# Context heads of three attention groups: transposed by VectorE in 32x32 blocks, their values summed on eight 32x64 tiles

## The chip, the cores and the metric

The kernel runs on one core of one Trainium2 chip. The metric is the device time of one execution in microseconds. The engines are named as the profile names them: PE is the matrix engine (PEld its weight loads), DVE the vector engine, ACT the scalar engine, POOL the GpSimd engine, and SP the engine that issues most DMAs.

## The reference

One layer of a diffusion transformer for 128 context tokens and 512 latent tokens, all float32, width 1024. Each of the two kinds of token is normalised and modulated, multiplied with one wide matrix `w_in`, and goes through grouped attention and a short gated convolution; then comes a gated feed-forward part. There are 16 query heads in 4 groups; the 4 heads of a group share one key and one value head of 64 columns. What matters here is the attention, and in it the context tokens, which read context tokens only:

```python
def block_attention(q, k, v):
    ...
    def one_block(qblk):
        s = jnp.einsum('bqkgd,btkd->bkgqt', qblk, k).astype(jnp.float32) * scale
        p = jax.nn.softmax(s, axis=-1).astype(v.dtype)
        return jnp.einsum('bkgqt,btkd->bqkgd', p, v)
    ...
# in the layer
h_p, k_ctx, v_ctx = trunk_layer(h_p, ada_ctx, p, None, None, None)
h_s, _, _ = trunk_layer(h_s, ada_lat, p, rope_tabs, cache_k[:, i], cache_v[:, i])
```

For a group the context part is thus four 128x128 score matrices (128 queries, 128 keys), a softmax over the keys, and four products with the same 128x64 matrix V. Latent queries read 640 keys: 128 cached ones and the 512 latent ones. The context's keys and values are outputs too (`new_k`, `new_v`).

## The kernel before

All 640 tokens (128 context, then 512 latent) are held on the chip with features on the partitions. Weights arrive in tiles of 128x1024 float32 (`raw`, three buffers) and are split into a rounded high part (ACT, `whi`) and the remainder (DVE, `wlo`), so that a product is three passes of the reduced-precision matmul (`mm3`, lines 157 to 159). Softmax weights and V are multiplied as plain float32, which the trace shows as two records for each matmul.

The attention stage goes over the groups `g` = 0 to 3, and in each over nine steps `i`. Step 0 makes the scores of the context heads (`Step(g)`, 4 heads, 128x128 each); steps 1 to 8 make those of two latent heads for 128 queries (`Step(g, place)`, two heads, 128x640 each, line 589). A step's scores are reduced to a maximum on DVE (`most`, lines 722, 727 and 729) and turned into exponentials with their sum on ACT (`exps`, lines 736 and 742); `shares` divides by the sum (reciprocal on DVE, lines 747 and 751; product on POOL, lines 748 and 752). One step later `turned` transposes the result on PE so that the keys lie on the partitions (context: line 760, latent: line 765), and a copy brings it from PSUM to the tile `PT` (line 762 on ACT, line 770 on ACT or DVE). `values` multiplies it with V (context: line 780, in step 2 of the group; latent: line 789, in steps 4, 6, 8 and step 1 of the next group), and its result is split into `AH` (ACT, line 794) and `AL` (DVE, line 795), the operands of the output projection.

The order of instructions on PE, ACT and DVE is the order in which the program writes them; the scheduler orders only SP and POOL and sets the waits and the buffers. In each step other PE work is written between the parts: half of a query projection for the next group (`q_part`), the other half, transposes of turned queries (`q_turn`, line 560), and modulation matmuls (`ada_mm`, line 209). Weight loads go through a ring (`ring_load`, lines 139 and 203) on SP. Remainders of the weights of the next projections are made in between on DVE (`cut_hi`, lines 690 and 693).

PSUM in this stage has two pools: `ps2()` gives tiles of two banks, of which there are three, and `ps1()` gives tiles of one bank, of which there are two:

```python
def ps2():
    return ps.tile([128, 1024], F32, tag="s2", name=nm("s2"), bufs=3)
def ps1():
    return psa.tile([128, 512], F32, tag="s1", name=nm("s1"), bufs=2)
```

The scores of a latent step take two tiles of `ps2`, those of the context step one; each transposed result takes one tile of `ps2`; `values` takes one of `ps1`. A tile is given again when the instructions that read it are done. `VV[:, 5]` holds V of the context tokens, with the 128 keys on the partitions and 4x64 columns for the four groups. `k_double(0)` also issues the DMAs that write `new_v` and `new_k` (lines 660 and 661).

Of the kernel before, what the change touches and what calls it, by code (L numbers as in the profile page):

```python
# [11 lines left out]
F32 = mybir.dt.float32  # L12
F32R = mybir.dt.float32r
AF = mybir.ActivationFunctionType
ALU = mybir.AluOpType
# [46 lines left out]
def trunk_layer(ctx, tc, x_prompt, x_sample, cache_k, cache_v, c, c_ctx, w_ada, b_ada, g_pre1, g_post1, g_pre2,  # L62
                g_post2, w_in, q_norm, k_norm, w_att_out, conv_w, w_conv_out, w_o, w_up, conv_ffn, w_down, rope,
                y_prompt, y_sample, new_k, new_v):
    nc = tc.nc
    V, S, G, PE = nc.vector, nc.scalar, nc.gpsimd, nc.tensor
# [17 lines left out]
    dp = ctx.enter_context(tc.tile_pool(name="dp", bufs=1, space=bass.MemoryType.DRAM))  # L84
# [7 lines left out]
    def nm(s):  # L92
        cnt[0] += 1
        return f"{s}_{cnt[0]}"

    def region(pool, tag, shape, dtype, name):
        return pool.tile([128] + shape, dtype, tag=tag, name=name)
# [6 lines that stand above are left out]
# [82 lines left out]
    scsh = const.tile([128, KT, 4], F32, name="scsh")  # L186
    mod = const.tile([128, 4, 2, KT], F32, name="mod")
    bct = dp.tile([64, 128], F32, name="bct")
    hd = dp.tile([NT, 128, D], F32, name="hd")
    actd = dp.tile([NJ, 128, NACT], F32, name="actd")  # L190

# [73 lines left out]
    with tc.tile_pool(name="pro", bufs=2) as pro, tc.manual_schedule(engines={mybir.EngineType.SP}):  # L265
# [122 lines left out]
        VV = kvp_.tile([128, 6, 256], F32, name="VV")  # L388
# [59 lines left out]
        for f in range(KT):  # L448
            g = {0: 2, 2: 3, 4: 4, 5: 5}.get(f - 1)
# [24 lines left out]
            if f + 1 < KT:  # L474
                g = {0: 1, 1: 2, 3: 3, 5: 4, 6: 5}.get(f)
# [6 lines left out]
            if f == KT - 3:  # L482
                V.tensor_scalar(out=gains[0], in0=gains[0], scalar1=HD ** -0.5, scalar2=None, op0=ALU.mult)
                for i in range(2):
                    for a in range(2):
                        V.tensor_tensor(out=tabs[i][:, :, 0, a * 32:a * 32 + 32], in0=rt[:, :, 0, a * 32:a * 32 + 32],
                                        in1=gains[i][:, :, a * 32:a * 32 + 32].broadcast_to((128, 4, 32)), op=ALU.mult)
                        for hf in range(2):
                            d0, s0 = a * 32 + hf * 16, a * 32 + (1 - hf) * 16
                            V.tensor_tensor(out=tabs[i][:, :, 1, d0:d0 + 16], in0=rt[:, :, 1, d0:d0 + 16],  # L490
                                            in1=gains[i][:, :, s0:s0 + 16].broadcast_to((128, 4, 16)), op=ALU.mult)
            if f == KT - 2:
                cut_upto(9)
                p = ps1()
# [10 lines left out]
    AH = region(ra, "r2", [KT, NTOK], F32R, "AH")  # L505
    AL = region(ra, "r3", [KT, NTOK], F32R, "AL")


    with tc.tile_pool(name="att", bufs=2) as at:
        def wide(shape, s="pr"):  # L510
            return at.tile(shape, F32, tag="pr", name=nm(s), bufs=4)
# [45 lines left out]
        def q_turn(g, t, p=None):  # L557
            p = ps1() if p is None else p
            for i in range(2):
                PE.transpose(p[:, i * 128:(i + 1) * 128], qfs[g, t][:, 2 * i:2 * i + 2].rearrange("p h d -> p (h d)"), ident)  # L560
            src = p[:, 0:256].rearrange("p (i c) -> p i c", i=2)
            qh, ql = (x[g][:, :, t * 128:(t + 1) * 128] for x in (QH, QL))
            S.activation(qh, src, AF.Copy)

            def low():
                V.tensor_tensor(out=ql, in0=src, in1=qh.bitcast(F32), op=ALU.subtract)
            return low
# [84 lines left out]
        def k_double(t):  # L652
            if t == 1:
                for i in range(2):
                    G.tensor_tensor(out=kds[t][:, :, i, :], in0=kfs[t], in1=rks[t].unsqueeze(2).broadcast_to((128, NKV, HD)), op=ALU.mult)
                return
            for h in range(NKV):
                S.activation(kds[t][:, h], kfs[t][:, h:h + 1, :].broadcast_to((128, 2, HD)), AF.Copy, scale=rks[t][:, h:h + 1])
            if t == 0:
                nc.sync.dma_start(new_v.rearrange("t h d -> t (h d)"), VV[:, 5, :])  # L660
                nc.sync.dma_start(new_k, kds[t][:, :, 0, :])

# [18 lines left out]
        PT = {}  # L681
# [4 lines left out]
        def cut_hi(i):  # L686

            raw = state["raw"][i]
            hi, lo = (wp.tile([128, 1024], F32R, tag=x, name=nm(x), bufs=3) for x in ("whi", "wlo"))
            S.activation(hi, raw, AF.Copy)  # L690

            def low(a=0, b=1024):
                V.tensor_tensor(out=lo[:, a:b], in0=raw[:, a:b], in1=hi[:, a:b].bitcast(F32), op=ALU.subtract)  # L693
                if b == 1024:
                    ring_used(1)
            state["cut"].append(Unit((hi, lo), units[i][4]))
            return low

        class Step:
# [54 lines left out]

            def turned(self, h):

                p = ps2()
                if self.ctx:
                    for i in range(4):
                        PE.transpose(p[:, i * 128:(i + 1) * 128], self.pr[:, i, :], ident)  # L760
                    dst = PT[self.g, "c"] = at.tile([128, 4, 128], F32, tag="PT", name=nm("PT"), bufs=3)
                    return lambda: S.activation(dst, p[:, 0:512].rearrange("p (h c) -> p h c", c=128), AF.Copy)
                qh, pi, qi = self.place
                for k in range(5):
                    PE.transpose(p[:, k * 128:(k + 1) * 128], self.pr[h][:, k * 128:(k + 1) * 128], ident)  # L765
                if qi == 0:
                    PT[self.g, qh, pi, h] = at.tile([128, 5, 256], F32, tag="PT", name=nm("PT"), bufs=3)
                dst = PT[self.g, qh, pi, h][:, :, qi * 128:(qi + 1) * 128]
                src = p[:, 0:640].rearrange("p (k c) -> p k c", c=128)
                return lambda v=False: V.tensor_copy(dst, src) if v else S.activation(dst, src, AF.Copy)  # L770

        def values(g, pair=None):

            vcol = slice(g * HD, (g + 1) * HD)
            pv = ps1()
            if pair is None:
                pt = PT.pop((g, "c"))
                for h in range(4):
                    o = 64 * (h % 2)
                    PE.matmul(pv[o:o + 64, (h // 2) * 128:(h // 2) * 128 + 128], VV[:, 5, vcol], pt[:, h, :], start=True, stop=True,  # L780
                              tile_position=(0, o))
                dst, lo = AH[:, 2 * g:2 * g + 2, 0:128], AL[:, 2 * g:2 * g + 2, 0:128]
                src = pv[:, 0:256].rearrange("p (h c) -> p h c", c=128)
            else:
                qh, pi = divmod(pair, 2)
                pts = [PT.pop((g, qh, pi, h)) for h in range(2)]
                for k in range(5):
                    for h in (0, 1):
                        PE.matmul(pv[64 * h:64 * h + 64, 0:256], VV[:, k, vcol], pts[h][:, k, :], start=k == 0, stop=k == 4,  # L789
                                  tile_position=(0, 64 * h))  # L790
                q0 = NCTX + qh * 256
                dst, lo = AH[:, 2 * g + pi, q0:q0 + 256], AL[:, 2 * g + pi, q0:q0 + 256]
                src = pv[:, 0:256]
            return (lambda: S.activation(dst, src, AF.Copy),
                    lambda: V.tensor_tensor(out=lo, in0=src, in1=dst.bitcast(F32), op=ALU.subtract))
# [15 lines left out]
        k_rotate(1)  # L811
        k_factors(4)
        k_double(0)
        k_copies(1)
        q_first(1)
# [4 lines left out]
        p = ps2()[:, 0:512]  # L820
# [4 lines left out]
        keep()  # L825
        q_rotate(pzs[1], 0, 1, V)
        k_double(2)
        k_done(0, p)
        sqs["q", 1] = squares(pzs[1])
        k_double(4)  # L830
        k_double(1)
        q_factors(1)
# [13 lines left out]
        low = q_turn(0, 2)  # L846
# [15 lines left out]
        for g in range(NKV):  # L862
            if g and g + 1 < NKV:
                q_begin(g + 1)
            for i in range(0 if g else 1, 9):
                low1, low2, late_hi, end = [], [], [], []
# [5 lines left out]
                    then = None  # L872
                if first:
                    low1.append(q_turn(*first))
                if i == 2:
                    hi, lo = values(g)
                    hi()
                    low1.append(lo)
                for h in range(1 if st.ctx else 2):
                    st.most(h)  # L880
                    st.exps(h)
                start, second = g == 0 and i == 1, g == 0 and i == 2
                if start:
                    low1.append(third)
# [11 lines left out]
                if i in (4, 6, 8) or (i == 1 and g):  # L896
                    hi, lo = values(*((g - 1, 3) if i == 1 else (g, (i - 4) // 2)))
                    late_hi.append(hi)
                    low2.append(lo)
# [31 lines left out]
                if (g, i) in CUTS:  # L931
                    low = cut_hi(CUTS[g, i])
# [51 lines left out]
        last.turned(1)()  # L984
        gate1_part(1, range(4))
        hi, lo = values(NKV - 1, 3)
        hi()
        lo()
# [21 lines left out]
    cut, raws, pair, TT = {}, {}, {}, {}  # L1010
# [293 lines left out]
    for j in range(KT):  # L1304
# [8 lines left out]
        _, hi, lo = cut["v", j]  # L1313
# [578 lines left out]
    w, x, y = NJ - 3, NJ - 2, NJ - 1  # L1892
# [85 lines left out]
```

## Time and profile before

| | |
|---|---|
| median of 3 runs | 1135.51 us (1134.22 to 1135.56) |
| span of the profiled execution | 1134.1 us; no other time is listed for it |
| mean granted PE clock | 0.996 |
| group 0 with its first step, 73.0 to 122.8 us | PE busy 46.20 of 49.80 us |
| group 1, 122.8 to 175.0 us | PE busy 52.20 of 52.20 us |
| group 2, 175.0 to 222.7 us | PE busy 47.70 of 47.70 us |
| group 3 and the end of the stage, 222.7 to 282.0 us | PE busy 59.25 of 59.30 us |

The page of the profile gives shares of the whole span, in which the attention stage is about a fifth; a change in it is read from the stretches of the stage and from the timeline. PE's matmuls are pipelined and their ends are modelled, so the time that a piece of PE work takes is read from start to start. "[1.98 <-ACT ...]" behind a row is the idle time of that engine before it, and what ended it.

### The profile page before, as it was taken

How to read it: one execution, taken by the hardware profiler on the slowest of the kernel's cores; microseconds unless marked ns; L12 is line 12 of the kernel's file. 1: busy time of each engine (PE TensorE's matmuls, PEld its weight loads, DVE VectorE, ACT ScalarE, POOL GpSimd, SP SyncE). 2: the span in 40 equal slices, each digit the busy share in tenths (PEclk: the TensorE clock that was granted, in tenths of full speed). 3: DMA queues.
4: the chain of work that ended last, by engine and by line, in shares of the span. 5: the costliest groups of instructions: out<-in, count | busy, mean ns of one | idle time of the engine just before them, and what ended most of it. 6: DMA issues, size and time to landing. Idle time of an engine off the chain costs nothing.

```text
span 1134.1 us, 19512 instructions
## 1 busy us (share of the span) xinstructions
PE 1114.9 (98%) x7885; PEld 1024.5 (90%) x7885; DVE 796.3 (70%) x1269; ACT 569.9 (50%) x979; POOL 158.9 (14%) x198
## 2 busy tenths in 40 slices
PE   7999999999999999999999999999999999999997
PEld 6787888888999999999999889999999999998786
DVE  4587666654656798889645458888788778888544
ACT  4375666665234444545522256655554545555431
POOL 2056566652000000000000012000000000002001
PEclk9999999999999999999999999999999999999999
DMA  9632433333222223223332644233333323315732
GB/s 335 205 92 82 126 94 112 110 96 112 76 75 75 75 77 105 81 75 95 93 111 76 207 164 150 76 99 99 98 112 109 95 91 109 105 61 186 240 99 93
DMA packets 177304, 129.58 MB, mean 114 GB/s; under 512 B 6274, under 2 KB 159422, under 8 KB 177214
## 3 DMA queue, kind: packets, MB, share of 16 engines
q1 hardware_dynamic: 177102, 128.30, 36.4%
q8 instruction: 62, 1.02, 0.4%
q14 instruction: 28, 0.23, 0.1%
q10 hardware_dynamic: 112, 0.04, 0.0%
HBM read 116.87 MB, written 11.45 MB: 113 GB/s over the span
## 4 chain that ended last, share of the span: by engine, by line
PE 89%; DVE 3%; ACT 1%; POOL 0%; issue 0%; DVEq 0%; POOLq 0%; ACTq 0%
PE b L1030 45%; PE b L159 9%; PE b L157 9%; PE b L158 9%; PE s L789 3%; PE s L765 3%; PE s L589 3%; PE s L157 2%; PE s L159 2%; PE s L158 2%; PE s L209 1%; DVE Y L1514 1%; DVE wlo L693 0%; PE s L560 0%; PE b L1421 0%; DVE mx L727 0%
## 5 line engine op out<-in xcount | busy, mean ns | idle before, releaser
L1030 PE MATMUL b<-ZB,whi 128*128 128x322 f32 x1024 | 228.6, 310 | 0.0
L1030 PEld LDWEIGHTS b<-ZB,whi 128*128 128x128 f32 x1024 | 173.8, 189 | 1.6
L1030 PE MATMUL b<-ZB,wlo 128*128 128x322 f32 x512 | 159.4, 311 | 0.0
L1030 PE MATMUL b<-MT,whi 128*128 128x320 f32 x608 | 134.1, 308 | 0.0
L1030 PEld LDWEIGHTS b<-MT,whi 128*128 128x128 f32 x608 | 101.7, 188 | 0.0
L1030 PEld LDWEIGHTS b<-ZB,wlo 128*128 128x128 f32 x512 | 96.2, 188 | 0.0
L1030 PE MATMUL b<-MT,wlo 128*128 128x320 f32 x304 | 93.8, 308 | 0.0
L752 POOL TENSOR_TENSOR pr<-pr,sm 128x640 f32<-128x640 f32 x64 | 80.7, 1270 | 61.1 <-DVE sm L751 61.1
L1017 ACT ACTIVATE whi<-SUM 128x1024 fp32r<-128x1024 f32 x40 | 42.2, 1055 | 79.6 <-DVE SUM L1484 77.2
L1514 DVE SCALAR_TENSOR_TENSOR Y<-C,cffn,Y 128x642 f32<-128x642 f32 x88 | 80.8, 920 | 0.9
L742 ACT ACTIVATE pr<-s,mx,rq 128x640 f32<-128x640 f32 x64 | 56.7, 886 | 38.5 <-DVE mx L729 36.4
L132 DVE TENSOR_TENSOR wlo<-raw,whi 128x1024 fp32r<-128x1024 f32 (+1 forms) x32 | 34.9, 1090 | 52.3 <-ACT whi L131 51.8
L1030 PE MATMUL b<-UH,whi 128*128 128x320 f32 x228 | 70.5, 309 | 0.0
L1030 PE MATMUL b<-UL,whi 128*128 128x320 f32 x228 | 70.4, 309 | 0.0
L1030 PE MATMUL b<-UH,wlo 128*128 128x320 f32 x228 | 70.2, 308 | 0.0
L1021 DVE TENSOR_TENSOR wlo<-raw,whi 128x1024 fp32r<-128x1024 f32 (+1 forms) x51 | 50.4, 1019 | 25.2 <-ACT whi L1017 24.3
L1017 ACT ACTIVATE whi<-WB 128x1024 fp32r<-128x1024 f32 x38 | 40.1, 1056 | 54.8 <-DVE WB L1125 54.8
L157 PE MATMUL s<-whi,UH 128*128 128x256 f32 (+1 forms) x200 | 65.8, 329 | 0.5 <-ACT UH L376 0.4
L727 DVE TENSOR_REDUCE mx<-s 128x1 f32<-128x640 f32 x64 | 52.5, 820 | 17.5 <-PE s L589 17.2
L158 PE MATMUL s<-wlo,UH 128*128 128x256 f32 (+1 forms) x200 | 61.5, 308 | 2.2 <-DVE wlo L693 2.2
L1038 ACT ACTIVATE p<-b 128x322 f32<-128x322 f32 (+1 forms) x78 | 34.3, 439 | 58.2 <-PE b L1030 58.2
L159 PE MATMUL s<-whi,UL 128*128 128x256 f32 (+1 forms) x200 | 61.8, 309 | 0.3
(322 smaller groups left out, 2933.0 us busy)
## 6 DMA issues: line engine op xcount, KB each, us to landing
raw<-in_w_in_dram SPq DMA_DIRECT2D x48, 512.0 KB, 3.6
RAW<-in_w_up_dram SPq DMA_DIRECT2D x40, 512.0 KB, 3.8
raw<-in_w_ada_dram SPq DMA_DIRECT2D x32, 512.0 KB, 4.0
raw<-in_w_down_dram SPq DMA_DIRECT2D x22, 512.0 KB, 4.2
actd<-Y SPq DMA_DIRECT2D x18, 321.0 KB, 2.5
AFB<-actd SPq DMA_DIRECT2D x18, 321.0 KB, 6.8
XT<-in_w_ada_dram SPq DMA_DIRECT2D x9, 512.0 KB, 8.5
raw<-in_w_conv_out_dram SPq DMA_DIRECT2D x9, 512.0 KB, 4.1
```

What stands on the lines that cost most here:

```text
L132: eng.tensor_tensor(out=lo[:, :n], in0=raw, in1=hi[:, :n].bitcast(F32), op=ALU.subtract)
L157: PE.matmul(out, ah, bh, start=start, stop=False)
L158: PE.matmul(out, ah, bl, start=False, stop=False)
L159: PE.matmul(out, al, bh, start=False, stop=stop)
L727: V.tensor_reduce(out=mx, in_=self.sc[h], axis=AX.X, op=ALU.max, negate=True)
L742: S.activation(pr, self.sc[h], AF.Exp, bias=mx, scale=rs, accum_out=sm)
L752: G.tensor_tensor(out=pr, in0=pr, in1=sm.broadcast_to((128, NTOK)), op=ALU.mult)
L1017: S.activation(to[0], raw, AF.Copy)
L1021: V.tensor_tensor(out=lo, in0=raw, in1=hi.bitcast(F32), op=ALU.subtract)
L1030: PE.matmul(out, p[:, ws], q[:, k, :], start=start and k == 0 and n == 0, stop=stop and k == 3 and n == 2, skip_group_check=True)
L1038: S.activation(t, pair[j][b], AF.Copy)
L1514: V.scalar_tensor_tensor(out=y, in0=crows(j)[i][:, d:d + NACT], scalar=cffn[:, 44 * d + o:44 * d + o + 1], in1=y, op0=ALU.mult, op1=ALU.add)
```

## The change

For groups 0, 1 and 2 the context heads take another way; group 3 keeps the old one.

`turned` issues one DVE transpose of the 128x512 tile, which turns each block of 32x32 by itself and writes `PT` directly; the PE transposes and ACT's copy are not issued, and no PSUM tile is taken. In the result, partition 32i + a holds, for the 32 queries of quadrant i, the weights of key 32j + a, with the key block j along the columns.

For that layout V is needed with key 32j + a on partition 32i + a, for each i: V is written to memory (`vd`) and read back four times into `VR`, which lies in the part of `AL` that belongs to group 3 and is written only later. The five DMAs are issued on SP in `k_double(0)`, ahead of those for `new_v` and `new_k`.

`values` then issues 32 matmuls with 32 rows, 64 weight columns and 64 moving columns (two heads of 32 queries): for each key block j, the four partition quadrants i, and the two halves h of the output partitions. Each quadrant i has its own PSUM bank; the four banks are two tiles of `ps2`. The split into `AH` and `AL` is done in two halves. In step 2 the call of `values` and the high part stand behind the step's maxima and exponentials instead of ahead of them.

```diff
@@ -186,6 +186,7 @@
     scsh = const.tile([128, KT, 4], F32, name="scsh")
     mod = const.tile([128, 4, 2, KT], F32, name="mod")
     bct = dp.tile([64, 128], F32, name="bct")
+    vd = dp.tile([128, 256], F32, name="vd")
     hd = dp.tile([NT, 128, D], F32, name="hd")
     actd = dp.tile([NJ, 128, NACT], F32, name="actd")
 
@@ -506,6 +507,8 @@
     AL = region(ra, "r3", [KT, NTOK], F32R, "AL")
 
 
+    VR = AL[:, 6:8, :].rearrange("p k c -> p (k c)")[:, 0:1024].bitcast(F32).rearrange("p (j c) -> p j c", j=4)
+
     with tc.tile_pool(name="att", bufs=2) as at:
         def wide(shape, s="pr"):
             return at.tile(shape, F32, tag="pr", name=nm(s), bufs=4)
@@ -657,6 +660,9 @@
             for h in range(NKV):
                 S.activation(kds[t][:, h], kfs[t][:, h:h + 1, :].broadcast_to((128, 2, HD)), AF.Copy, scale=rks[t][:, h:h + 1])
             if t == 0:
+                nc.sync.dma_start(vd, VV[:, 5, :])
+                for i in range(4):
+                    nc.sync.dma_start(VR[32 * i:32 * i + 32], vd.rearrange("(j a) c -> a j c", a=32))
                 nc.sync.dma_start(new_v.rearrange("t h d -> t (h d)"), VV[:, 5, :])
                 nc.sync.dma_start(new_k, kds[t][:, :, 0, :])
 
@@ -754,6 +760,9 @@
 
             def turned(self, h):
 
+                if self.ctx and self.g < 3:
+                    dst = PT[self.g, "c"] = at.tile([128, 4, 128], F32, tag="PT", name=nm("PT"), bufs=3)
+                    return lambda: V.transpose(dst.rearrange("p h c -> p (h c)"), self.pr.rearrange("p h c -> p (h c)"))
                 p = ps2()
                 if self.ctx:
                     for i in range(4):
@@ -772,6 +781,27 @@
         def values(g, pair=None):
 
             vcol = slice(g * HD, (g + 1) * HD)
+            if pair is None and g < 3:
+                pt = PT.pop((g, "c")).rearrange("p (i h) (j b) -> p h j i b", h=2, b=32)
+                pq = [ps2() for _ in range(2)]
+                for j in range(4):
+                    for i in range(4):
+                        rows = slice(32 * i, 32 * i + 32)
+                        for h in range(2):
+                            PE.matmul(pq[i // 2][64 * h:64 * h + 64, 512 * (i % 2):512 * (i % 2) + 64], VR[rows, j, vcol], pt[rows, h, j],
+                                      start=j == 0, stop=j == 3, tile_position=(32 * i, 64 * h))
+                dsts, lows = ([x[:, 2 * g:2 * g + 2, 64 * n:64 * n + 64].rearrange("p i (q b) -> p q i b", b=32) for n in range(2)]
+                              for x in (AH, AL))
+                srcs = [p.rearrange("p (q c) -> p q c", q=2)[:, :, 0:64].rearrange("p q (i b) -> p q i b", b=32) for p in pq]
+
+                def high():
+                    for n in range(2):
+                        S.activation(dsts[n], srcs[n], AF.Copy)
+
+                def low():
+                    for n in range(2):
+                        V.tensor_tensor(out=lows[n], in0=srcs[n], in1=dsts[n].bitcast(F32), op=ALU.subtract)
+                return high, low
             pv = ps1()
             if pair is None:
                 pt = PT.pop((g, "c"))
@@ -872,13 +902,17 @@
                     then = None
                 if first:
                     low1.append(q_turn(*first))
-                if i == 2:
+                if i == 2 and g == 3:
                     hi, lo = values(g)
                     hi()
                     low1.append(lo)
                 for h in range(1 if st.ctx else 2):
                     st.most(h)
                     st.exps(h)
+                if i == 2 and g < 3:
+                    hi, lo = values(g)
+                    hi()
+                    low1.append(lo)
                 start, second = g == 0 and i == 1, g == 0 and i == 2
                 if start:
                     low1.append(third)
```

## The prediction

> **What bounds the kernel now.** I read the page first, then the windows of the stage that the change touches, then the waits of TensorE in it, then the timeline at the places that are edited.
>
> ```profile
> PE 1114.9 (98%) x7885; PEld 1024.5 (90%) x7885; DVE 796.3 (70%) x1269; ACT 569.9 (50%) x979; POOL 158.9 (14%) x198
> PE 89%; DVE 3%; ACT 1%; POOL 0%; issue 0%; DVEq 0%; POOLq 0%; ACTq 0%
> 73.00:122.80 49.80, 46.20 (x475) 38.22 (x473) 37.54 (x95) 33.10 (x73) 30.86 (x32) 1.00 0.22 65
> 122.80:175.00 52.20, 52.20 (x570) 43.92 (x563) 35.73 (x94) 33.69 (x73) 32.85 (x34) 1.00 0.36 109
> 175.00:222.70 47.70, 47.70 (x518) 39.64 (x516) 31.31 (x88) 31.86 (x69) 28.69 (x30) 1.00 0.35 104
> PE s L158 <- DVE wlo L693: 2.2, 2, 1.2
> PE s L765 <- POOL pr L752: 0.8, 1, 0.8
> PE s L589 <- ACT pr L742: 0.3, 1, 0.3
> PE s L393 <- DVE KL L400: 0.2, 1, 0.2
> ```
>
> TensorE is the bound of the whole (98% busy, 89% of the chain that ended last). The next three rows are the stage of attention groups 0, 1 and 2 (stretch, its length, then PE, PEld, DVE, ACT, POOL busy, clock, DMA share). In groups 1 and 2 PE is busy for all of 52.20 and 47.70 us: a microsecond given to or taken from PE there counts in full. Group 0 is another case: 3.6 us of idle PE in 49.80, and the waits (PE, 70 to 283 us) put nearly all of it on its first three steps, behind DVE, POOL and ACT. So the sum is made twice: by PE time in groups 1 and 2, by the VectorE chain in group 0. Group 3 keeps the old path.
>
> **The change in a dense group.** Group 1, from the context heads' transposes to the step that uses their result (start, duration, engine, line):
>
> ```profile
> 131.42 0.16 DVE L751 RECIPROCAL sm<-sm 128x1 f32<-128x1 f32 x1 [0.20 <-ACT pr L742]
> 131.53 0.66 PE L760 MATMUL s<-ident,pr 128*128 128x128 f32 x4
> 131.66 2.47 POOL L752 TENSOR_TENSOR pr<-pr,sm 128x640 f32<-128x640 f32 x2 [2.07 <-DVE sm L751]
> 132.11 1.08 PE L209 MATMUL s<-raw,s 128*32 128x128 f32 x32
> 132.28 0.60 ACT L762 ACTIVATE PT<-s 128x512 f32<-128x512 f32 x1
> 132.35 0.17 DVE L751 RECIPROCAL sm<-sm 128x1 f32<-128x1 f32 x1 [0.77 <-ACT pr L742]
> 133.81 0.31 PE L589 MATMUL s<-KL,QH 64*128 64x320 f32 x2
> 133.96 0.31 PE L589 MATMUL s<-KH,QL 64*128 64x320 f32 x2
> 134.20 0.66 PE L780 MATMUL s<-PT,VV 128*64 128x128 f32 x8
> 134.30 0.82 DVE L727 TENSOR_REDUCE mx<-s 128x1 f32<-128x640 f32 x1 [0.18 <-PE s L589]
> 134.79 0.39 PE L157 MATMUL s<-whi,UH 128*128 128x256 f32 x1
> 134.90 0.39 ACT L794 ACTIVATE AH<-s 128x256 fp32r<-128x256 f32 x1 [1.75 <-PE s L780]
> 135.43 0.89 ACT L742 ACTIVATE pr<-s,mx,rq 128x640 f32<-128x640 f32 x1
> L722 DVE TENSOR_REDUCE mxc<-s x4: 677/678/679, 74.6 to 224.4; 128x4 f32<-128x512 f32 x4
> ```
>
> *Removed.* Four PE transposes (L760): from their start to that of what follows, 132.11 - 131.53 = 0.58 us of PE. Eight records of the value matmuls (L780): 134.79 - 134.20 = 0.59 us. On ACT the 0.60 copy of PT goes; ACT is idle much of the time here (1.75 before L794), so that is worth nothing.
>
> *Added on DVE.* One 128x512 transpose, placed behind the reciprocal of 131.42. No row shows that operation. Its nearest is the reduction over 128x512, 0.68 us; it would run from 131.58 to 132.26 and end just before the next reciprocal at 132.35, for which DVE waits 0.77 anyway. From below it could take nothing that matters, since DVE idles there. From above: beside POOL's L752 a 128x512 subtraction of VectorE took up to 1.74 (the second of L693's two, below, is the bound for this). Then it ends near 133.3, and what follows it on DVE (reciprocal, the low part of AL, a sum, the maxima of the next scores) is up to 0.9 late, which would lengthen the wait below by as much. I take 0, since the transpose has one SBUF input, like the reduction, and keep 0.9 for the range.
>
> *Added on PE.* 32 matmuls, 64 records by the two records for each that L780 shows (4 matmuls, x8), with 64 columns instead of 128. Four column tiles side by side are in L209: 32 records of 128 columns in 1.08, about (1.08 - 0.27)/7 = 0.116 for each four, so 0.058 for 64 columns. Two row tiles side by side are in L589: a pair every 133.96 - 133.81 = 0.15. Eight tiles at once, four rows by two columns, are in no row. All eight at once: 64/8 x 0.058 = 0.46. Four at once: 0.93. Only the column pair that L780 shows: 32 x 0.065 = 2.1. I take 0.7, between the first two, as both kinds of tile overlap separately.
>
> *The wait that comes in.* This is the largest term. The old value matmuls wrote a one-bank tile of the pool of two. The new ones write two tiles of the two-bank pool that has three slots. The running step's scores hold two of the three until their exponentials have read them. So the first new tile (query quadrants 0 and 1) finds a slot, and the second (quadrants 2 and 3), whose matmuls come fifth in PE's order, has to wait for exponential 0 of the same step. That fits with the edit's other half, which moves the values behind the maxima and exponentials. PE works in order: behind the waiting matmul stand the query projection's L157 to L159 and both transposes. From the last pair of scores to the end of that exponential: 135.43 + 0.89 - 133.96 = 2.36. To reach PE it takes 0.14 more (exponential at 80.51 + 0.89 = 81.40, scores at 81.54; rows below).
>
> So from 133.96: 2.36 + 0.14, then seven eighths of 0.7 us, 0.6, then 0.2 of changeover (as between the last scores' 133.96 + 0.15 and 134.20), 3.3 us, where before it was 134.79 - 133.96 = 0.83. Longer by 2.5, shorter by the transposes' 0.58: **+1.9 us** in each of groups 1 and 2. The bounds are +1.4 (tiles at 0.46, no changeover) and +4.2 (tiles at 2.1, DVE late by 0.9). Nothing gives it back: in these groups PE waits for no other engine, and the chain stays on PE.
>
> ACT and DVE get two halves of 128x128 each where one 128x256 was (0.39 and 0.42), about 0.27 each by the 0.60 for 512 columns. They stand behind exponential 1 now, and behind them stand ACT's and DVE's copies of PT; DVE has idle time before its next due copy, and PE's transposes are late by the same 1.9. I cost that at nothing in these groups.
>
> **The change in group 0.** Here DVE sets the pace, and the row order is what matters:
>
> ```profile
> 80.51 0.89 ACT L742 ACTIVATE pr<-s,mx,rq 128x640 f32<-128x640 f32 x1
> 81.54 0.41 PE L589 MATMUL s<-KH,QH 64*128 64x320 f32 x1 [0.26 <-ACT pr L742]
> 82.59 0.82 DVE L727 TENSOR_REDUCE mx<-s 128x1 f32<-128x640 f32 x1 [0.20 <-PE s L589]
> 84.07 0.89 ACT L742 ACTIVATE pr<-s,mx,rq 128x640 f32<-128x640 f32 x1 [0.36 <-DVE mx L729]
> 85.17 0.41 DVE L795 TENSOR_TENSOR AL<-s,AH 128x256 fp32r<-128x256 f32 x1
> 85.34 0.89 ACT L742 ACTIVATE pr<-s,mx,rq 128x640 f32<-128x640 f32 x1 [0.29 <-DVE mx L729]
> 86.59 3.45 POOL L752 TENSOR_TENSOR pr<-pr,sm 128x640 f32<-128x640 f32 x2
> 87.11 3.47 DVE L693 TENSOR_TENSOR wlo<-raw,whi 128x1024 fp32r<-128x1024 f32 x2
> 88.97 0.39 PE L158 MATMUL s<-wlo,UH 128*128 128x256 f32 x1 [1.09 <-DVE wlo L693]
> 92.36 0.68 DVE L693 TENSOR_TENSOR wlo<-raw,whi 128x512 fp32r<-128x512 f32 x1
> ```
>
> The transpose of 0.68 goes into a DVE that is nearly full; against it, scores of step 2 find a slot one exponential sooner (they waited for the one that ends at 81.40) and the 0.58 of PE transposes is gone, so the maxima still start near 82.6 to 82.7. The context's low part (L795), which ended at 85.58, now waits for exponential 1 (85.34 + 0.89 = 86.23), its read-out and the two copies to AH, and ends near 87.5: 1.9 later. DVE's copy of PT, the low part of Q and L693 follow. Some comes back: the two L693 ran beside POOL's 3.45 and took 3.47 for 1024 and 512 columns, where one of 512 alone took 0.68, so later pieces are up to about 0.7 faster in all. Net **+1.3 us**, with bounds of +0.3 and +2.3.
>
> **V in four quadrants.** SP writes V to memory and reads it back four times, ahead of the writes of new_v and new_k and of two weight loads:
>
> ```profile
> actd<-Y SPq DMA_DIRECT2D x18, 321.0 KB, 2.5
> 66.69 0.37 SPq L139 DMA_DIRECT2D raw<-in_w_in_dram  x1
> 67.18 26.34 SPq L203 DMA_DIRECT2D raw<-in_w_ada_dram  x3
> 87.22 1.06 ACT L690 ACTIVATE whi<-raw 128x1024 fp32r<-128x1024 f32 x1
> ```
>
> The reads wait for the write's landing, 2.5 by the nearest row, then four issues of about 0.4: the two loads behind them move by 1 to 4 us from 66.69. The first is read at 87.22, the other in a later step, and SP has issues with 20 us between them after that. V's copies land near 70, against their first use after 82. This costs nothing; without that cover of 15 us it would be up to 4 us.
>
> **The clock.** The stall makes a hole of some 2.1 us in PE twice, and of 2.8 in group 0 (82.3 to 85.1). The one hole of that size in the old trace is this:
>
> ```profile
> 1051.74 0.50 PE L157 MATMUL b<-WD,ACTa 128*128 128x512 f32 x1 [1.98 <-ACT ACTa L1529]
> 1052.80:1056.00 3.20, 3.20 (x8) 2.55 (x9) 2.50 (x5) 2.06 (x6) 0.00 (x0) 0.50 1.02 398
> ```
>
> After 1.98 us of waiting the granted clock was 0.50 for some 3.4 us. On a stretch bound by PE that is 1.7 us lost. The holes of 1.1 and 1.2 at 88.97 and near 93 left group 0 at 1.00. The Trainium skill, "TensorE: Matmul & The Clock Gate", section "Why this matters for your kernels", says that gaps up to about 3 us do not lower the clock; by that the sum would get nothing, and by the row up to 3 x 1.7. The row differs from the rule in one case only, and a hole has to fall well inside one of the clock's stretches, so I leave it out of the likeliest sum and make it a rival.
>
> **Sum.** 1.3 + 1.9 + 1.9 = +5.1 us on the profiled span of 1134.1, hence 1139.2; the median of the runs lies 1.4 above the span, so 1140.6.
>
> **Rivals.**
> 1. *The holes drop the clock.* For: 1.98 us did it once. Against: shorter holes did not, and each of the new ones has full-size matmuls around it. One to three events: 1142.3 to 1145.7. Chance 0.28.
> 2. *The eight tiles do not run side by side.* For: no row shows them. Against: rows and columns each do. At 2.1 us instead of 0.7, 1.2 more in groups 1 and 2 and some 0.8 in group 0: 1143.8. One at a time, 4.2, would give about 1149. Chance 0.12.
> 3. *Not slower: the second tile finds a slot without a wait,* because the scores of the step are given up sooner than I think. Then each dense group gains 0.58 + 0.59 and pays 0.7 and little else, -0.5, and group 0 stands still: 1134.5, no measurable change. It decides in a dense group at a wait of about 0.5 us; I count 2.1 by a chain of maximum, product and exponential that no edit shortens. Chance 0.09.
>
> **How the numbers follow.** About 0.2% (2.3 us) is what a measurement of this kernel can tell from no change. The forecast holds 0.46, and 0.05 is left for mishaps on either side. The low end is the sum of the small bounds, 0.3 + 1.4 + 1.4 = 3.1, less a little: 1138.0. The high end takes in three clock events and the pair-only tiles: 1146.0. Outside are rival 3, one-at-a-time tiles and part of the rest. Slower by over 0.2%: forecast, rivals 1 and 2 and most of the rest, 0.89; the same 0.08; faster 0.03.
>
> **What would show it.** In groups 1 and 2 of the new trace: no L760 transposes there, a DVE transpose of about 0.7 us, four (eight records) value matmuls, then a PE wait of about 2 us that ends by ACT's L742, and a dense rest; waits of PE for ACT's exponentials of 4 to 6 us in all, where 0.3 stood. In group 0 the wait for L693 moves, and step 3 starts a microsecond or so late. I am wrong if PE shows no wait behind the scores of step 2, if 64 records take over 1 us, if the transpose takes over 1.3 and holds the maxima, or if the clock's row shows 0.50 in this stage.

## The result, and the profile after

The changed kernel takes 1141.07 us (median of 3 runs, 1141.03 to 1144.04) against 1135.51: a ratio of 1.0062, with a 95% interval of 1.0041 to 1.0083. Its profiled execution has a span of 1139.2 us, against 1134.1.

The page's first part and chain:

```profile
PE 1115.3 (98%) x8041; PEld 1025.6 (90%) x8041; DVE 797.1 (70%) x1275; ACT 568.3 (50%) x979; POOL 157.6 (14%) x198
PE 88%; DVE 3%; ACT 1%; issue 0%; DVEq 0%; POOLq 0%; ACTq 0%; POOL 0%
```

PE is busy for as long as before, in a span that is 5 us longer. The waits of PE, 70 to 290 us, in the trace after:

```profile
PE s L791 <- ACT pr L748: 6.4, 3, 2.6
PE s L158 <- DVE wlo L699: 0.9, 2, 0.7
PE s L791 <- ACT sq L532: 0.5, 1, 0.5
```

L791 are the tiled value matmuls, L748 the exponentials: three waits, one in each changed group. Group 1 after, in order of time:

```profile
133.10 0.69 DVE L765 STREAM_TRANSPOSE PT<-pr 128x512 f32<-128x512 f32 x1
133.13 1.08 PE L210 MATMUL s<-raw,s 128*32 128x128 f32 x32
134.98 0.31 PE L592 MATMUL s<-KH,QL 64*128 64x320 f32 x2
135.22 0.34 PE L791 MATMUL s<-PT,AL 32*64 32x64 f32 x8
135.33 0.82 DVE L733 TENSOR_REDUCE mx<-s 128x1 f32<-128x640 f32 x1 [0.16 <-PE s L592]
136.46 0.88 ACT L748 ACTIVATE pr<-s,mx,rq 128x640 f32<-128x640 f32 x1 [2.27 <-DVE mx L735]
137.49 0.85 PE L791 MATMUL s<-PT,AL 32*64 32x64 f32 x56 [1.92 <-ACT pr L748]
138.27 0.39 PE L157 MATMUL s<-whi,UH 128*128 128x256 f32 x1
```

Eight records go to the first tile, then PE stands until the exponential of 136.46 has ended at 137.34; 0.15 later the other 56 run, and L157 follows 3.29 us after the last scores.

The stage by groups, each from its first context scores to those of the next (length, PE, PEld, DVE, ACT, POOL busy, granted clock, DMA share, GB/s); first before, then after. The window of group 1 in the table ahead of the prediction (to 175.0) runs 2.3 us into group 2; PE is busy throughout in both, so nothing that was read from it changes.

```profile
73.17:122.88 49.71, 46.11 (x474) 38.19 (x474) 37.45 (x94) 33.01 (x73) 30.83 (x32) 1.00 0.22 65
122.88:172.74 49.86, 49.86 (x542) 41.73 (x539) 33.43 (x91) 32.83 (x72) 30.68 (x32) 1.00 0.35 107
172.74:222.62 49.88, 49.88 (x544) 41.75 (x540) 33.46 (x91) 32.57 (x71) 30.70 (x32) 1.00 0.36 107
```

```profile
73.04:124.49 51.45, 47.17 (x525) 39.46 (x525) 36.52 (x96) 32.55 (x73) 29.85 (x32) 0.97 0.24 69
124.49:176.21 51.72, 49.80 (x594) 41.81 (x590) 34.21 (x93) 32.28 (x72) 30.66 (x32) 1.00 0.35 103
176.21:229.48 53.27, 51.35 (x596) 43.37 (x592) 34.24 (x93) 32.03 (x71) 30.68 (x32) 0.97 0.34 100
```

The groups are longer by 1.74, 1.86 and 3.39 us, 7.0 in all. Group 3, which is unchanged, is as long as before, 60.5. Groups 0 and 2 have a clock of 0.97: in each a stretch at half clock lies right behind the hole in PE. The same windows, after, the stretch with the hole and the one behind it, for groups 0, 1 and 2:

```profile
81.70:84.90 3.20, 0.34 (x8) 0.23 (x8) 3.06 (x7) 1.96 (x4) 3.20 (x4) 1.00 0.00 0
85.00:88.30 3.30, 3.19 (x66) 3.03 (x67) 1.29 (x5) 1.35 (x4) 2.46 (x4) 0.50 0.00 0
133.00:136.10 3.10, 2.57 (x54) 1.90 (x52) 2.66 (x7) 1.19 (x3) 2.67 (x4) 1.00 0.31 80
136.30:139.50 3.20, 2.01 (x66) 1.95 (x67) 1.50 (x6) 2.29 (x6) 0.99 (x2) 1.00 0.79 234
187.40:190.70 3.30, 1.50 (x62) 1.43 (x63) 1.89 (x6) 2.29 (x6) 1.26 (x3) 1.00 0.94 282
190.80:194.10 3.30, 3.30 (x18) 3.30 (x17) 0.80 (x3) 1.06 (x1) 1.25 (x1) 0.50 0.03 7
```

In groups 0 and 2 the hole lies inside one stretch (PE busy 0.34 of 3.20, 1.50 of 3.30), and the next runs at 0.50. In group 1 the hole of 1.92 is split over two stretches (the second starts at 136.17), and the clock stays.

The span grew by 5.1 and not by 7.0 because the two traces also differ behind the stage. Before, PE had its own half-clock stretch at 1052.7, shown in the prediction; after, the clock is up from the stretch in group 2 nearly to the end:

```profile
194.30:1136.20 941.90, 935.95 (x6176) 878.13 (x6174) 670.81 (x946) 457.25 (x737) 71.48 (x91) 1.00 0.34 106
```

Such stretches come and go from one execution to the next (the mean clock of the kernel before is 0.994 to 0.999 in its executions), so the lengths of the groups are a cleaner measure of the change than the span.

### The profile page after: what moved, and what is told of

Same layout as the page of the kernel before. It is cut to its first block, busy times and chain, and to the rows that moved or that the text cites. A ratio compares the mean times of both kernels' runs of the same rounds, so it can differ in the third digit from the quotient of the medians.

```text
span 1139.2 us, 19835 instructions
## 1 busy us (share of the span) xinstructions
PE 1115.3 (98%) x8041; PEld 1025.6 (90%) x8041; DVE 797.1 (70%) x1275; ACT 568.3 (50%) x979; POOL 157.6 (14%) x198
## 4 chain that ended last, share of the span: by engine, by line
PE 88%; DVE 3%; ACT 1%; issue 0%; DVEq 0%; POOLq 0%; ACTq 0%; POOL 0%
PE b L1064 45%; PE b L159 9%; PE b L157 9%; PE b L158 9%; PE s L819 3%; PE s L774 3%; PE s L592 3%; PE s L157 2%; PE s L159 2%; PE s L158 2%; PE s L210 1%; DVE Y L1548 1%; DVE mx L733 1%; ACT pr L748 0%; PE s L563 0%; PE b L1455 0%
## 5 line engine op out<-in xcount | busy, mean ns | idle before, releaser
L748 ACT ACTIVATE pr<-s,mx,rq 128x640 f32<-128x640 f32 x64 | 56.6, 885 | 42.0 <-DVE mx L735 40.2
L157 PE MATMUL s<-whi,UH 128*128 128x256 f32 (+1 forms) x200 | 66.3, 331 | 0.6 <-ACT UH L377 0.4
```

What stands on the lines that cost most here:

```text
L157: PE.matmul(out, ah, bh, start=start, stop=False)
L748: S.activation(pr, self.sc[h], AF.Exp, bias=mx, scale=rs, accum_out=sm)
```

## The experiments

All are compared with the kernel before (median near 1135.5 in every comparison).

**e1_late: the tiled matmuls later in PE's order.**

```diff
-                if i == 2 and g < 3:
-                    hi, lo = values(g)
-                    hi()
-                    low1.append(lo)
...
                     q_part(pz, *qt, range(KT - 2, KT))
+                if i == 2 and g < 3:
+                    hi, lo = values(g)
+                    hi()
+                    low2.append(lo)
```

> The changed kernel with one edit: the tiled value matmuls of groups 0, 1 and 2 stand behind the second half of the query projection of step 2, so that both exponentials of the step are done and PE has other work in between. Theory (PE waits for the second two-bank tile until exponential 0 has read the scores): the wait of 1.9 us in groups 1 and 2 and of 2.6 in group 0 goes, no row of PE waiting for L748 ahead of the tiled matmuls over 0.3 us; each dense group then is 0.58 + 0.59 of removed PE work less 0.98 of new, so 0.2 under the kernel before, group 0 within 0.7 of it: 1134.5 to 1136.5. Rival (the tiled matmuls themselves, or the transposes on DVE, are what costs): nothing of that is moved, so 1139.5 to 1141.5. Rival (the half clock behind the holes is most of it): also back to before, but then the experiment that fills the holes must fall as far.

Measured: 1138.57 us, ratio 1.0033 (1.0023 to 1.0043). The groups are longer than before by 0.25, 1.25 and 1.23 us. Group 0, two of PE's waits, and the place in group 1:

```profile
73.29:123.25 49.96, 45.96 (x527) 38.19 (x526) 36.53 (x96) 32.63 (x73) 29.79 (x32) 1.00 0.24 71
PE s L592 <- ACT PT L779: 2.7, 2, 1.4
PE s L791 <- ACT pr L748: 0.6, 1, 0.6
137.59 0.91 PE L791 MATMUL s<-PT,AL 32*64 32x64 f32 x64
138.43 0.44 PE L563 MATMUL s<-ident,qf 128*128 128x128 f32 x2
140.78 0.48 PE L592 MATMUL s<-KH,QH 64*128 64x320 f32 x2 [1.36 <-ACT PT L779]
```

The wait for the exponentials is gone in groups 1 and 2 (0.6 is left in group 0, where PE now waits 2.34 us for POOL ahead of the transposes), and the 64 records run in one piece. But a wait of 1.36 us has come up at the next scores, which want two of the same three tiles. The expected time was missed, and that of the rival too: only part of the loss went. The low part of AL, which frees the new tiles, stood in DVE's order behind the turned queries' low part, which waits for ACT; e5 takes that away.

**e2_order_only: the old value matmuls in the new place.**

```diff
-                if i == 2:
+                if i == 2 and g == 3:
                     hi, lo = values(g)
...
                     st.exps(h)
+                if i == 2 and g < 3:
+                    hi, lo = values(g)
+                    hi()
+                    low1.append(lo)
```

> The kernel before with one edit: in groups 0, 1 and 2 the old value matmuls and their high part are written behind the maxima and exponentials of step 2, as the change has it; transposes, copies and tiles are the old ones. Theory (the wait is for the slot of the two-bank pool): the old result lies in the one-bank pool, PE waits for nothing new, and ACT's and DVE's two short instructions come 1 to 2 us later; 1135.5, within 0.7 either way, group 0 perhaps 0.5 later since DVE is full there. Rival (the order alone, with the low part of AL late on DVE, costs): 1138 to 1141.

Measured: 1136.41 us, ratio 1.0005 (0.9997 to 1.0014), no difference that can be told. By groups (windows of e2):

```profile
73.11:123.50 50.39, 46.63 (x473) 38.31 (x473) 36.93 (x94) 33.18 (x73) 30.78 (x32) 1.00 0.22 64
123.50:173.34 49.84, 49.84 (x542) 41.74 (x539) 33.44 (x91) 32.38 (x71) 31.07 (x32) 1.00 0.35 107
PE s L560 <- DVE AL L795: 1.0, 1, 1.0
```

The order alone costs nothing in the dense groups and 0.68 us in group 0, where PE's transposes of the turned queries now wait for DVE's late low part of AL.

**e3_fill: the holes filled with useless matmuls.**

```diff
                 if i == 2 and g < 3:
+                    junk = ps1()[:, 0:256]
+                    for n in range(16 if g else 22):
+                        PE.matmul(junk, UH[:, 0, 0:128], UH[:, 0, 0:256], start=True, stop=True)
                     hi, lo = values(g)
```

> The changed kernel with useless work added: ahead of the tiled value matmuls of groups 0, 1 and 2 PE gets 22, 16 and 16 matmuls of 128x256 into an unused one-bank tile, 1.8 to 2.4 us, about as long as the hole. Their result is read by nothing. Theory (two causes, the wait by itself and, only sometimes, a half-clock window of 3.4 us behind it): the stage from group 0 to group 3 shows no clock of 0.50, the waits of PE for L748 shrink to under 0.6 each, and the time is that of the change less 1.7 for each window that it had: about 1139, 1138 to 1140.5. Rival (half the loss or more is the clock in every execution): 1136.5 to 1138. Rival (the clock does not matter): 1141 or a little above, as the change.

Measured: 1138.64 us, ratio 1.0031 (1.0019 to 1.0042): 2.4 us under the change's median with 54 more matmuls (the intervals of the two ratios to before overlap by 0.0001). Windows and a piece of group 1's timeline of e3:

```profile
73.29:123.83 50.54, 48.69 (x547) 40.85 (x547) 36.57 (x96) 32.52 (x73) 29.83 (x32) 1.00 0.25 71
123.83:175.54 51.71, 51.71 (x610) 43.73 (x607) 34.22 (x93) 32.31 (x72) 30.66 (x32) 1.00 0.35 103
175.54:227.26 51.72, 51.72 (x612) 43.75 (x608) 34.24 (x93) 32.05 (x71) 30.69 (x32) 1.00 0.35 103
134.56 2.17 PE L915 MATMUL s<-UH 128*128 128x256 f32 x16
136.66 1.01 PE L791 MATMUL s<-PT,AL 32*64 32x64 f32 x64
```

The clock is 1.00 in all three groups, and groups 1 and 2 are equal at 51.7. This takes the loss apart: without the half clock a dense group is 1.85 us longer than before, which group 1 of the change (1.86, clock 1.00) confirms, and group 0 is 0.83 longer, 4.5 in all. The half-clock stretches added 51.45 - 50.54 = 0.9 to group 0 and 53.27 - 51.72 = 1.5 to group 2 of the profiled change.

**e4_double: the 32 matmuls issued twice.**

```diff
-                for j in range(4):
+                for j in (0, 1, 2, 3, 0, 1, 2, 3):
```

> The changed kernel with the 32 tiled value matmuls of each of groups 0, 1 and 2 issued twice (the second set starts over, so the result is the same). Theory (the matmuls are a small term, about 0.8 us a set, and the wait is the large one): 0.7 to 0.9 more in groups 1 and 2 and up to 0.9 in group 0, 2 to 2.6 in all: 1143 to 1143.7, the waits as before. Rival (the tiles and their modes are the main cost, 2 us a group): 4 to 6 more, 1145 to 1147.

Measured: 1145.07 us, ratio 1.0087 (1.0074 to 1.0101). The total is 1.4 above what the theory gave and lies at the low end of the rival's range, so the time alone does not decide; the trace does. The three groups together are 2.53 us longer than in the profiled change, as the theory had it (2 to 2.6); the rest of the longer span lies outside the stage, where this execution has a half-clock stretch at 1063 that the change has not. In group 0 the clock was 0.94, where the change had 0.97, and that group is 1.2 longer (52.67 against 51.45). In group 1, where it is 1.00 in both kernels, the second set adds 52.39 - 51.72 = 0.67 us:

```profile
126.05:178.44 52.39, 50.47 (x658) 42.49 (x654) 34.21 (x93) 32.35 (x72) 30.65 (x32) 1.00 0.34 102
139.05 1.53 PE L791 MATMUL s<-PT,AL 32*64 32x64 f32 x120 [1.93 <-ACT pr L748]
80.20:83.60 3.40, 2.08 (x25) 1.57 (x23) 3.26 (x12) 2.83 (x6) 2.49 (x4) 1.00 0.00 0
83.60:87.00 3.40, 1.65 (x109) 1.65 (x115) 1.80 (x3) 1.95 (x4) 3.03 (x4) 0.50 0.00 0
```

64 more records take 1.53 - 0.85 = 0.68 us, and the wait is as it was. The tiles are not the main cost. The last two rows are group 0: its hole of 2.57 us (82.78 to 85.35) is split at 83.60, and here the clock fell all the same.

**e5_late_low: as e1, the low part at once.**

```diff
                     hi()
-                    low2.append(lo)
+                    lo()
```

> As e1_late, but the low part of AL is written right behind the high part, ahead of the turned queries' low part, so that DVE does not hold both new tiles until ACT has made the next weights' high part. Theory (the pool of three two-bank tiles is the whole matter: in e1_late the wait moved to the next scores, 1.36 us behind ACT's copy of PT, since the new tiles were still held): the wait of PE at the scores of step 3 in groups 1 and 2 goes, and a dense group stands 0.3 under to 0.2 over the kernel before; group 0 is 0.3 to 0.8 over it by its full DVE; 1135 to 1136.6. Rival (one wait always comes back, or the tiled matmuls cost more than the 1.17 us that was removed): 1137.5 to 1139, as e1_late.

Measured: 1138.13 us, ratio 1.0026 (1.0014 to 1.0037). The wait at the scores is gone, and a dense group is 0.48 over the kernel before (windows, waits and timeline of e5):

```profile
73.14:124.25 51.11, 48.02 (x525) 40.29 (x524) 36.41 (x96) 32.64 (x73) 29.86 (x32) 0.93 0.24 71
124.25:174.60 50.35, 50.07 (x596) 41.76 (x592) 34.19 (x93) 32.04 (x72) 30.71 (x32) 1.00 0.35 106
PE s L774 <- POOL pr L758: 2.3, 1, 2.3
PE s L157 <- DVE QL L569: 0.3, 2, 0.2
138.59 0.91 PE L791 MATMUL s<-PT,AL 32*64 32x64 f32 x64
139.44 0.44 PE L563 MATMUL s<-ident,qf 128*128 128x128 f32 x2
144.45 0.28 PE L157 MATMUL s<-whi,UH 128*128 128x256 f32 x1
144.81 0.39 PE L158 MATMUL s<-wlo,UH 128*128 128x256 f32 x1
```

The expected gain did not come, though the tiles by themselves bring one. From start to start the 64 records take 0.85 us (138.59 to 139.44), and about 0.14 goes to the changeovers on both sides: 0.99, or 0.18 less than the 1.17 that was removed. Two small waits of PE take more than that: 0.15 for the turned queries and some 0.24 for a weight's low part (144.45 to 144.81, where one matmul takes 0.12), 0.55 together with PE's slower restart behind them. In group 0 the hole moved to the transposes, which wait 2.3 us for POOL, and the clock fell there for two stretches (0.93). Group 0 of e1 has the same hole, the clock stayed at 1.00 and the group was only 0.25 longer than before, where this one is 1.40 longer; so most of that is the clock. The time lies outside what the theory gave and inside the rival's range.

**e6_late_low_12: the same for groups 1 and 2 alone.**

```diff
-                if self.ctx and self.g < 3:
+                if self.ctx and self.g in (1, 2):
...
-            if pair is None and g < 3:
+            if pair is None and g in (1, 2):
...
-                if i == 2 and g == 3:
+                if i == 2 and g not in (1, 2):
...
-                if i == 2 and g < 3:
+                if i == 2 and g in (1, 2):
```

> As e5_late_low, but group 0 keeps the old transposes, copies and matmuls in their old place; only groups 1 and 2 are changed (V is still copied into four quadrants). Theory (group 0's loss comes from its order and its full DVE): its loss is nil, so the time is that of the kernel before less at most 0.6: 1134.9 to 1135.8. Rival (what e5_late_low loses, if anything, is in the dense groups): the same as e5_late_low.

Measured: 1136.24 us, ratio 1.0005 (0.9996 to 1.0013). Group 0 is back at 49.72, groups 1 and 2 stand at 50.35 as in e5: no measurable difference in the medians, and no gain. It is 0.4 above what the theory gave: group 0's loss is nil, as expected, but the dense groups keep their 0.48 each. Executions with the same mean clock show these: at 0.999 the four spans of e6 are 1133.0 to 1133.3 us, the five of the kernel before 1132.3 to 1132.4.

**e7_transpose_twice: DVE's transpose issued twice.**

```diff
-                    return lambda: V.transpose(dst.rearrange("p h c -> p (h c)"), self.pr.rearrange("p h c -> p (h c)"))
+                    def twice():
+                        for _ in range(2):
+                            V.transpose(dst.rearrange("p h c -> p (h c)"), self.pr.rearrange("p h c -> p (h c)"))
+                    return twice
```

> The changed kernel with DVE's transpose issued twice in groups 0, 1 and 2. Theory (in the dense groups the single transpose of 0.69 us hides in DVE's idle time before the next reciprocal, with 0.16 to spare): the second pushes reciprocal, sums and maxima back by some 0.5, and so the exponential that PE waits for: 0.3 to 0.6 in each of groups 1 and 2, up to 0.7 in group 0; 1142 to 1143, with as many half-clock windows as in the change. Rival (the first transpose is not hidden either): a full 0.7 in each group. Rival (DVE has room for both): the time of the change.

Measured: 1143.29 us, ratio 1.0073 (1.0058 to 1.0089). In the dense groups my expectation was wrong and the second rival right (e7, group 1; group 2 is 51.72 long):

```profile
126.31:178.06 51.75, 49.83 (x595) 41.84 (x592) 34.59 (x94) 32.04 (x71) 30.75 (x32) 1.00 0.34 103
```

Both are as long as group 1 of the change: DVE has room for two transposes of 0.69 before the maxima are due. Group 0 became 1.9 longer than in the change (53.34 against 51.45), with a longer hole (3.0 us) and a clock of 0.94: there DVE has no room, and the exponential that ends the hole starts at 85.13 instead of 83.98.

**e8_dma_only: the five DMAs added to the kernel before.**

```diff
             if t == 0:
+                nc.sync.dma_start(vd, VV[:, 5, :])
+                for i in range(4):
+                    nc.sync.dma_start(VR[32 * i:32 * i + 32], vd.rearrange("(j a) c -> a j c", a=32))
                 nc.sync.dma_start(new_v.rearrange("t h d -> t (h d)"), VV[:, 5, :])
```

> The kernel before with the five DMAs that write V to memory and read it into four quadrants, whose result nothing reads; all else is old. Theory (the 15 us up to the first use of the loads behind them cover it): 1135.5, within 0.7, every step of the stage within 0.2 of its old time. Rival (SP's wait for the write delays the next weights): up to 4 us more in the first steps of group 0.

Measured: 1135.87 us, ratio 1.0005 (0.9996 to 1.0015). The groups are 49.71, 49.88 and 49.86 long, as before. SP's issues in e8:

```profile
61.38 0.34 SPq L663 DMA_DIRECT2D vd<-VV  x1
65.80 2.26 SPq L665 DMA_DIRECT2D AL<-vd  x4
69.39 0.40 SPq L139 DMA_DIRECT2D raw<-in_w_in_dram  x1
```

The weight load moved from 66.69 to 69.39, and nobody waited for it.

## Why the prediction was right, and where not

*The wait for the second tile: right, in place, cause and size.* The hole was put at some 2.1 us and ended by the exponential; the trace has 1.92 in each dense group, ended by L748. Once the matmuls stand behind other PE work, that wait is gone (e1), and with the tiles freed early most of the dense loss is (e5, 1.85 to 0.48), while the order alone (e2) and the DMAs (e8) cost these groups nothing. That the pool of three tiles is the cause is also shown by where e1's loss went: to the next user of the same pool.

*The dense sum: right.* From the last scores to L157 3.3 us was worked out and 3.29 measured; +1.9 for a group against 1.86. One reading in it is off: the row named for the changeover gives 134.20 - 133.96 - 0.15 = 0.09, not 0.2. The 0.2 was right all the same: the last 56 records took 0.78 to the next matmul, and seven eighths of 0.67 are 0.59. The bounds come out as +1.5 and +4.0 by the terms given, not +1.4 and +4.2, which changes nothing.

*The eight tiles: right within the bounds.* A set of 64 costs 0.67 (e4), where 0.7 was chosen between 0.46 (eight at once) and 0.93 (four at once). So rival 2 falls.

*The transpose: right in duration, and in being hidden in the dense groups.* 0.69 against 0.68, and the same beside POOL's product. The reason given, one SBUF input like the reduction, does not fit: that reduction reads the scores, which are in PSUM. The slack was judged too small: I thought it ended just before something that was due, and e7 shows room for another. In group 0 it is not hidden: PE starts the first tile at 82.10, 0.1 after the transpose has ended, with a wait of 0.51 that the view puts down to ACT; with two transposes (e7) this wait is 1.25.

*Group 0: direction right, path and size wrong.* +1.3 was summed; without a half-clock stretch it is +0.83 (e3). The prediction let DVE carry the delay, by the context's low part of AL, to end near 87.5. It ended at 86.92, PE waited for none of it, and DVE stood idle before and behind it (1.33, 0.68 and 1.38 us, behind ACT and PE). The delay goes through PE's own order: behind its wait for the second tile stand the transposes, the rest of the projection and the scores of step 3. Counted from the group's first scores, those of step 3 start at 13.20 before and at 15.46 in e3, 2.26 later, where 1.9 was taken. More came back as well: I took 0.7 from L693, by its slowness beside POOL. After, the two ran behind POOL's products and took 1.89 in place of 3.47, and PE's two waits for L693 fell from 2.25 to 0.76 in e3, by 1.49. 2.26 less 1.49 is 0.77, near the 0.83 that was measured; the two wrong terms cancel in part. The rows after:

```profile
86.43 0.49 DVE L803 TENSOR_TENSOR AL<-s,AH 128x128 fp32r<-128x128 f32 x2 [1.33 <-ACT AH L799]
88.71 1.25 POOL L758 TENSOR_TENSOR pr<-pr,sm 128x640 f32<-128x640 f32 x1 [0.33 <-DVE sm L757]
90.29 1.89 DVE L699 TENSOR_TENSOR wlo<-raw,whi 128x1024 fp32r<-128x1024 f32 x2
91.56 0.39 PE L158 MATMUL s<-wlo,UH 128*128 128x256 f32 x1 [0.68 <-DVE wlo L699]
```

The order alone costs 0.68 in e2, but by a wait of PE for the low part of AL that the changed kernel does not have, so it is no share of the 0.83.

*The clock: a rival that came true, and one of the named signs of being wrong.* I left it out of the likeliest sum and gave it 0.28. In the profiled change it happened twice and cost some 2.4 us, 0.9 and 1.5 where I had priced 1.7 each (e3). By the Trainium skill, "TensorE: Matmul & The Clock Gate", section "Why this matters for your kernels", PE should have no idle gaps of more than about 3 us; here holes of 1.92 and 2.57 us were followed by 0.50, so staying under that bound is not enough, and the measurement decides. Part 1 of that page of the Trainium skill describes a free-running window of about 3.4 us. The trace agrees: the two stretches at 0.50 last 3.41 us each and start at 84.97 and 190.78, 105.81 us apart, which is 31 times 3.413. Group 1's hole, as long as that of group 2 but split over two windows, did no harm, nor did the split hole of 2.34 in group 0 of e1; the one in group 0 of e4 did. How much idle time in a window is too much is therefore not shown exactly.

*The total: right, partly by accident.* 1140.6 was forecast and 1141.07 measured; the spans agree to 0.1 us. But the stage lost 7.0 in the profiled execution, where I had 5.1: 4.5 by the waits (group 0 smaller than forecast) and 2.4 by the clock. Then 1.8 came back behind the stage, since the old trace had lost some of it to a half-clock stretch of its own. The waits of PE for the exponentials came to 6.4, a little over the 4 to 6 that was named. Rival 3, no wait and no loss, falls with the 1.92.

Where the stretches lie in the executions that were not profiled isn't known, but the mean clock of each is. In the change it is 0.996 twice, with spans of 1139.2 and 1139.3 us, and 0.991 once, with 1142.2. By an estimate from these figures, a loss of 0.004 of 1139 us is some 9 us at half clock, about the two stretches of 3.4 and the last 3 us of the profiled span, which also ran at 0.50; 0.991 means about three stretches more. So all three executions had such stretches, somewhere in the span. The clock also explains why e3's median is only 3.1 above before, where its groups are 4.5 longer: five of its six executions have 0.997 to 0.999. At 0.999 alone its spans are 1136.5 and 1136.9, those of the kernel before 1132.2 to 1133.0 (five executions), 4.4 apart by their middles.

## What to carry to other kernels

When a step is moved to other buffers, count the tiles of that pool that are alive at the place where it stands in the order, and see who frees the next: the work taken off the bounding engine was worth nothing here, because the new result wanted two tiles where one was free. Even with that mended (e5), a saving of 0.18 us a group was less than the small waits that the new order brought. A wait that is moved away can come back at the next user of the same pool, so free the tiles at once. Price a hole in PE with the clock behind it as well as with its own length, and compare executions of the same mean clock where a difference is small.

## What the runs showed of the hardware that was not expected

- Holes of 1.92 and 2.57 us in PE that lay inside one of the clock's stretches of 3.4 us were each followed by a whole stretch at half clock, which cost 1.5 us where PE is the bound and 0.9 in group 0. Split over two stretches, a hole did no harm in two cases and lowered the clock in one (e4). With the holes filled by useless matmuls the clock stayed up in all three groups.
- Eight 32x64 tiles, four row groups by two column groups, overlap: 64 float32 records of 64 columns take 0.67 us, about 10 ns each, between the estimates of 0.46 for eight at once and 0.93 for four.
- VectorE's transpose of a 128x512 float32 tile in 32x32 blocks takes 0.69 us, as long as a reduction over as many elements (0.68).
